# Two buffer changes in a two-layer trunk: narrow PSUM banks for every second pair of v, and GpSimd making both parts of eighteen weights

## The chip, the cores and the metric

The kernel runs on one core of a Trainium2 chip. The metric is device time in microseconds (us) of one execution, from the chip; lower is better. The core has a matrix engine (TensorE, PE in the profile; its weight loads are PEld), VectorE (DVE), ScalarE (ACT), GpSimd (POOL) and a sync engine that issues the DMAs (SP). Each engine runs its own queue in order and waits on semaphores for the others. Matmul results land in PSUM, eight banks of 128 partitions x 512 fp32; GpSimd doesn't touch PSUM in this kernel.

## The reference

The input is one sequence of 1024 tokens with 1024 features, all fp32. Two layers follow each other.

```python
def _dsa_mixer(x, ...):                 # layer 0
    q, c_kv, q_idx, k_idx, w_idx, z = split(x @ w_in)
    c_kv = rmsnorm(c_kv)
    # per block of 128 queries: score all causal keys, keep the best 256
    idx_score = einsum(w_idx, relu(q_idx @ k_idx.T)); sel = top_k(idx_score, 256)
    p = softmax(q_lat . c_kv[sel] - slope * distance)
    return ((p . c_kv[sel]) @ w_uv * silu(z)) @ w_out

def _mlstm_mixer(x, ...):               # layer 1
    qk, v, ig, fg, o, z = split(x @ w_in)
    # causal conv and silu on qk, then a chunked recurrence with gates ig, fg over q, k, v
    return (sigmoid(o) * rmsnorm(h) * silu(z)) @ w_out

# each layer: x = layernorm(alpha * x + mixer(x))
```

## The kernel before

Every large product is made in three passes of a rounded fp32 format (fp32r). `mm3` (lines 58 to 61) multiplies a high part h and a low part l of each operand: h·h, h·l and l·h. The high part is a rounded copy of the fp32 value, the low part is the value minus the high part. So each weight that arrives by DMA is split twice: a copy that makes h, and a subtract that makes l. `split_sb` (line 54) puts the copy on ScalarE and the subtract on VectorE, or on an engine that is given.

`load_w` (line 63) does this for the weights of the first layer: a DMA from the sync queue into `w_st` (line 67, two buffers), a ScalarE copy into `w_h` (line 68, three buffers) and a subtract into `w_l` (line 69, three buffers) on VectorE or, with `pool_l=True`, on GpSimd. `pool_l` is true for eighteen weights of 128x1024: eight for z (`z_unit`), two for the key/value latent (`ckv_a`) and eight for q (`q_unit`). Five others (`w_idx1` and four of `load_u`) use VectorE.

The first layer has three stages that matter here. In the first, TensorE makes the index scores of six query blocks (`scores`), and the z, latent and q projections (`proj_T`). At the same time the top 256 keys of each block are found by a search bit by bit (`sel_step`): for each of 32 bits and each group of blocks, one pass over the scores M counts how many reach a candidate value, and two tiny VectorE instructions (lines 269 and 270) move the candidate. Groups a, b and c (blocks 7, 6 and 5) count on ScalarE (line 253), groups d and e (blocks 4, 3 and 2) on VectorE (line 256). `sel_final` (lines 280 to 308) then turns the scores of each group into a mask in M. The third stage, attention (`soft`, `attend`), reads the masks. Between them `k_unit` and `v_piece` make keys and values of the first pair of heads.

The second layer begins with the v projection. `v_unit` (line 721) makes plain stretches of columns: its weights come in by DMA and are split (`split_sb`), then four pairs of token blocks (the loop over `tp`) are multiplied into PSUM, each block is copied as `vh` (ScalarE, line 758), subtracted as `vl` (VectorE, line 759) and written to DRAM from the two buffers of `VE`. It is called three times: columns 1792 to 2056 (264 wide, gates included), 1024 to 1536 (512 wide) and 1536 to 1792 (256 wide). `v_unit7` makes the other half of v after it.

PSUM has two kinds of tiles: `ps_a` has one bank and four buffers ("narrow"), `ps_y` has two banks and two buffers ("wide"). All plain units of v use `ps_y`. Around them `ps_a` holds the transposes `xt` of the norm (line 590) and the transposed gates `yg` (line 635, two banks, read by lines 640 and 645).

The order on each engine is not written out by hand up to line 1123: a planner places instructions by their dependences, their place in the program and its own estimate of durations, and chooses when a buffer is given out. By hand is only the later part (`manual_schedule`, pairs and the recurrence).

Of the kernel before, what the change touches and what calls it, by code (L numbers as in the profile page):

```python
# [14 lines left out]
AF = mybir.ActivationFunctionType  # L15
# [15 lines left out]
def trunk(ctx, tc, I, out):  # L31
    nc = tc.nc
    PE, DVE, ACT, POOL, SP = nc.tensor, nc.vector, nc.scalar, nc.gpsimd, nc.sync
# [8 lines left out]
    def ps_a(name="pa"):  # L42
        return ps.tile([128, 512], F32, name=name, tag="a", bufs=4)

    def ps_y(name="py"):
        return ps.tile([128, 2, 512], F32, name=name, tag="y", bufs=2)

    def slab(name, dt=F32, shape=(128, 1024)):
        return xp.tile(list(shape), dt, name=name, tag="x", bufs=16)

    def f32(ap):
        return ap.bitcast(F32)

    def split_sb(src, h, l, eng=None):
        ACT.activation(h, src, AF.Copy)  # L55
        (eng or DVE).tensor_tensor(l, src, f32(h), op=OP.subtract)  # L56

    def mm3(o, sh, sl, mh, ml, start, stop):
        PE.matmul(o, lhsT=sh, rhs=mh, start=start, stop=False)  # L59
        PE.matmul(o, lhsT=sh, rhs=ml, start=False, stop=False)  # L60
        PE.matmul(o, lhsT=sl, rhs=mh, start=False, stop=stop)  # L61

    def load_w(src, shape, pool_l=False):
        st = wp.tile(list(shape), F32, name="w_st", tag="st", bufs=2)
        h = wp.tile(list(shape), F32R, name="w_h", tag="wh", bufs=3)
        l = wp.tile(list(shape), F32R, name="w_l", tag="wl", bufs=3)
        SP.dma_start(st[:], src)
        ACT.activation(h[:], st[:], AF.Copy)  # L68
        (POOL if pool_l else DVE).tensor_tensor(l[:], st[:], f32(h[:]), op=OP.subtract)  # L69
        return h, l  # L70

# [54 lines left out]
    for k in range(8):  # L126
        xs = ap_.tile([128, 1024], F32, name="xs", tag="p", bufs=4)
        st = wp.tile([128, 456], F32, name="w_st", tag="st", bufs=2)
        wh = wp.tile([128, 456], F32R, name="w_h", tag="wh", bufs=3)
        wl = wp.tile([128, 456], F32R, name="w_l", tag="wl", bufs=3)  # L130
        h, l = slab("xh", F32R), slab("xl", F32R)
# [17 lines left out]
    def proj_T(src, pool_l=False):  # L149

        wh, wl = load_w(src, [128, 8, 128], pool_l)
        y = ps_y()
        for k in range(8):
            for hf in range(2):
                s = slice(hf * 512, hf * 512 + 512)
                mm3(y[:, hf, :], wh[:, k, :], wl[:, k, :], xh[k][:, s], xl[k][:, s], k == 0, k == 7)
        return y[:].rearrange("p a b -> p (a b)")
# [24 lines left out]
    for c in range(2):  # L182
        y = yq[c][:].rearrange("p a b -> p (a b)")
        stack_q(c, [(y[:, 256:1024], 256, 768)])
    stack_q(2, [(aq[0][0][:, 256:512], 256, 256), (aq[0][1][:, :], 512, 512)])
    y = proj_T(I["w_idx1"])
# [13 lines left out]
    for b in range(2):  # L200
        n = 128 * (b + 1)
# [115 lines left out]
    def ckv_a():  # L317
        w = [load_w(I["w_ckv"][i], [128, 4, 256], True) for i in range(2)]
        for tp in range(4):
            if tp % 2 == 0:  # L320
                ckf.append(ap_.tile([128, 4, 256], F32, name="ckf", tag="z", bufs=2))
            a = ps_a("ck")
            for j in range(2):
                t = slice((2 * tp + j) * 128, (2 * tp + j) * 128 + 128)
                for k in range(8):
                    wh, wl = w[k // 4]
                    mm3(a[:, j * 256:j * 256 + 256], xh[k][:, t], xl[k][:, t], wh[:, k % 4, :],
                        wl[:, k % 4, :], k == 0, k == 7)
            o = (tp % 2) * 2
            ACT.activation(ckf[-1][:, o:o + 2, :], a[:].rearrange("p (j c) -> p j c", j=2), AF.Copy)  # L330
            for j in range(2):
                ACT.activation(a[:, j * 256:j * 256 + 256], ckf[-1][:, o + j, :], AF.Square,
                               accum_out=ckss[:, 2 * tp + j:2 * tp + j + 1])
# [32 lines left out]
    def load_u(p):  # L366
        uw[p] = load_w(I["w_ukv"][p], [128, 2, 2, 256])
# [178 lines left out]
    for k in range(8):  # L546
        st = wp.tile([128, 1024], F32, name="w_st", tag="st", bufs=2)
        SP.dma_start(st[:], I["a_w_out"][k])
        h, l = slab("woh", F32R), slab("wol", F32R)
# [3 lines left out]
    def x2tile(name, dt=F32R):  # L553
        return x2p.tile([128, 4, 512], dt, name=name, tag="x2", bufs=8)
# [13 lines left out]
    for b in range(NB):  # L568
# [7 lines left out]
        y = ps_y("yo")  # L576
        for h, hf in ([(h, hf) for h in range(8) for hf in range(2)] if b < 2 else
                      [(h, hf) for hf in range(2) for h in range(8)]):
                n = slice(hf * 512, hf * 512 + 512)
# [7 lines left out]
        for c4 in range(2):  # L587
# [4 lines left out]
            for c in range(4):  # L592
                k = c4 * 4 + c
# [3 lines left out]
            h, l = (v[:, :, (b % 4) * 128:(b % 4) * 128 + 128] for v in X1[c4][b // 4])  # L597
# [123 lines left out]
    def v_unit(c0, c1, on_slabs):  # L721
        n = c1 - c0
        nv = min(c1, 2048) - c0
        w = []
        g = 1024 // n // 2 * 2 or 2
        for i in range(8 // g):
            st = wp.tile([128, g, n], F32, name="v_st", tag="st", bufs=2)
            SP.dma_start(st[:], I["w_vg"][:, g * i:g * i + g, c0:c1])
            if i < 3 and not on_slabs:
                wh = wp.tile([128, g, n], F32R, name="v_h", tag="wh", bufs=3)  # L730
                wl = wp.tile([128, g, n], F32R, name="v_l", tag="wl", bufs=3)
            else:
                wh, wl = (slab("v_x", F32R, (128, g, n)) for _ in range(2))
                if on_slabs:
                    XT.extend([wh, wl])
            split_sb(st[:], wh[:], wl[:])
            w += [(wh[:, j, :], wl[:, j, :]) for j in range(g)]
        if nv < n:
            G = slab("G", F32, (128, NB, 36))
            GC.append(G)  # L740
            POOL.memset(G[:, :, 4:32], 0.0)
        h, j0 = divmod(c0, 512)
        j0 //= 256
        nj = nv // 256
        js = slice(j0, j0 + nj)
        for tp in range(4):
            y = ps_y("yv")
            for j in range(2):
                tb = 2 * tp + j
                for k in range(8):  # L750
                    xh1, xl1 = (v[:, (tb % 4) * 128:(tb % 4) * 128 + 128] for v in x1[k][tb // 4])
                    mm3(y[:, j, :n], xh1, xl1, *w[k], k == 0, k == 7)
                if nv < n:
                    for i in range(2):
                        DVE.tensor_copy(G[:, tb, 32 * i:32 * i + 4], y[:, j, 256 + 4 * i:260 + 4 * i])
                vh, vl = VE[j]
                yv = y[:, j, :nv].rearrange("p (j n) -> p j n", j=nj)
                ACT.activation(vh[:, js, 0:256], yv, AF.Copy)
                DVE.tensor_tensor(vl[:, js, 0:256], yv, f32(vh[:, js, 0:256]), op=OP.subtract)
                for o, v in ((XH, vh), (XL, vl)):  # L760
                    o += 258 * j0
                    SP.dma_start(X_dram[h, tb, :, o:o + 258 * nj],
                                 f32(v[:, js, :].rearrange("p j n -> p (j n)")))
# [335 lines left out]

    W2 = {}  # L1100
    v_unit(1792, 2056, False)
    gates()
    gate_cols()
    v_unit(1024, 1536, True)
    XT += [slab("T", F32R, (128, 2, 512)) for _ in range(8)]
    right_factors(2)
    right_factors(3)
    right_factors(0)
    right_factors(1)
    v_unit(1536, 1792, False)  # L1110
    bctx.close()
    actx, sctx = ExitStack(), ExitStack()
# [26 lines left out]
    p = pairs[0]  # L1139
    for f in (p.prep0, p.prep1, p.prep2, p.prep3, p.s1, p.s2):  # L1140
        f()
    for n, p in enumerate(pairs[:-1]):
# [4 lines left out]
        if n == 19:  # L1147
            for k in (0, 2):
                st = x2tile("w2_st", F32)
# [318 lines left out]
```

## Time and profile before

| what | value |
|---|---|
| median of three runs | 1577.13 us (1575.67 to 1577.32) |
| profiled execution | 1580.19 us, its span 1578.1 us |
| mean granted TensorE clock | 0.989 |
| busy share of the span | PE 97%, PEld 83%, DVE 75%, ACT 55%, POOL 11% |

The profiled execution is 3.1 us above the median of the three runs, and 2.1 us of it lie outside the span (first to last instruction). "Busy" is the time in which an engine had an instruction under way; instructions overlap a little at their ends. A wait is given by the instruction that waited, the one that released it, and how long the engine sat idle. Times in the rows are us from the span's start.

### The profile page before, as it was taken

Reading aid. Unit: us, or ns where it says so; the run is one execution under the profiler, and the core shown is the slowest. Engines: PE = TensorE matmul, PEld = TensorE weight load, DVE = VectorE, ACT = ScalarE, POOL = GpSimd, SP = SyncE. Lnnn points to the kernel's source line nnn. Section 1 sums busy time; section 2 is a strip of 40 time slices with the busy share of each in tenths; the row PEclk is TensorE's granted clock in tenths of the full one; section 3 lists DMA queues with packets and bytes.
Section 4 is the critical chain, followed back from the end, with each engine's and each line's share of the span. In section 5 each row is a group of like instructions: output and inputs, shape, how many; then the busy total and the mean of one; then the engine's idle time right before and its main releaser. Section 6 shows DMA issues by size and latency. Waiting matters only on the chain.

```text
span 1578.1 us, 22430 instructions
## 1 busy us (share of the span) xinstructions
PE 1537.9 (97%) x8081; PEld 1312.4 (83%) x8081; DVE 1176.6 (75%) x2393; ACT 866.1 (55%) x1554; POOL 177.2 (11%) x158
## 2 busy tenths in 40 slices
PE   9999999999999999999999999999999999999997
PEld 6888888899998888887878888888888778888886
DVE  3569999887873558836788888987776677757876
ACT  3588887576775546222456464646565554344431
POOL 0212112044368300000000000000000000000000
PEclk9999999999999999999999999999999989999999
DMA  5121211111013335245746656574662476676551
GB/s 182 54 80 56 80 41 48 47 32 35 30 54 95 117 129 164 96 154 164 240 158 210 190 184 204 168 232 140 185 209 81 159 266 227 215 249 248 204 197 41
DMA packets 118510, 223.41 MB, mean 142 GB/s; under 512 B 9336, under 2 KB 66040, under 8 KB 114816
## 3 DMA queue, kind: packets, MB, share of 16 engines
q1 hardware_dynamic: 118400, 222.00, 42.8%
q8 instruction: 63, 1.03, 0.3%
q14 instruction: 47, 0.39, 0.1%
HBM read 148.40 MB, written 73.56 MB: 141 GB/s over the span
## 4 chain that ended last, share of the span: by engine, by line
PE 68%; DVE 19%; DMA 6%; ACT 4%; issue 3%; POOL 0%; SPq 0%; DVEq 0%; ACTq 0%; POOLq 0%
PE p L59 6%; PE p L61 6%; PE p L60 6%; PE yo L59 5%; PE yo L61 5%; PE yo L60 5%; DVE junk L256 3%; PE ys L59 2%; PE ys L61 2%; PE ys L60 2%; PE pt L471 2%; DVE M L224 2%; ACT junk L253 1%; DMA f_st<-in_w_vg_dram 1%; PE yl L59 1%
## 5 line engine op out<-in xcount | busy, mean ns | idle before, releaser
L59 PE MATMUL py<-xh,w_h 128*128 128x512 f32 x272 | 106.6, 392 | 1.6 <-ACT w_h L68 1.4
L61 PE MATMUL py<-xh,w_l 128*128 128x512 f32 x272 | 106.4, 391 | 0.0
L59 PE MATMUL yo<-wo,oh 128*128 128x512 f32 (+1 forms) x264 | 104.3, 395 | 2.1 <-ACT oh L55 2.0
L60 PE MATMUL py<-xl,w_h 128*128 128x512 f32 x272 | 106.1, 390 | 0.0
L61 PE MATMUL yo<-wo,ol 128*128 128x512 f32 (+1 forms) x264 | 103.9, 394 | 0.1
L60 PE MATMUL yo<-wo,oh 128*128 128x512 f32 (+1 forms) x264 | 103.8, 393 | 0.0
L59 PE MATMUL p<-x1h,p_h 128*128 128x512 f32 x192 | 75.6, 394 | 0.1
L61 PE MATMUL p<-x1h,p_l 128*128 128x512 f32 x192 | 74.8, 390 | 0.0
L60 PE MATMUL p<-x1l,p_h 128*128 128x512 f32 x192 | 74.8, 389 | 0.0
L56 DVE TENSOR_TENSOR p_l<-p_st,p_h 128x1024 fp32r<-128x1024 f32 x48 | 58.7, 1223 | 17.6 <-ACT p_h L55 17.5
L55 ACT ACTIVATE p_h<-p_st 128x1024 fp32r<-128x1024 f32 x48 | 50.6, 1055 | 32.9 <-PE p L60 26.6
L454 POOL TENSOR_SCALAR p<-p,sm 128x640 f32<-128x640 f32 (+2 forms) x24 | 58.3, 2437 | 70.6 <-DVE sm L453 57.2
L69 POOL TENSOR_TENSOR w_l<-w_st,w_h 128x1024 fp32r<-128x1024 f32 x18 | 44.3, 2466 | 192.8 <-ACT w_h L68 192.8
L55 ACT ACTIVATE p_h<-p_f 128x1024 fp32r<-128x1024 f32 (+1 forms) x48 | 40.4, 842 | 42.7 <-PE ys L60 20.3
L59 PEld LDWEIGHTS py<-xh,w_h 128*128 128x128 f32 x272 | 51.2, 188 | 12.5 <-ACT w_h L68 1.7
L61 PEld LDWEIGHTS yo<-wo,ol 128*128 128x128 f32 x264 | 50.4, 191 | 13.1 <-DVE ol L56 1.1
L59 PEld LDWEIGHTS yo<-wo,oh 128*128 128x128 f32 x264 | 50.3, 191 | 12.5 <-ACT oh L55 3.0
L1030 DVE SCALAR_TENSOR_TENSOR acc<-yq,conv_w,acc 128x1023 f32<-128x1023 f32 (+2 forms) x48 | 60.1, 1277 | 0.0
L61 PEld LDWEIGHTS py<-xh,w_l 128*128 128x128 f32 x272 | 51.3, 189 | 10.3
L60 PEld LDWEIGHTS py<-xl,w_h 128*128 128x128 f32 x272 | 51.2, 188 | 10.3
L55 ACT ACTIVATE Ch<-Cf 128x516 fp32r<-128x516 f32 x56 | 35.6, 635 | 43.7 <-DVE Cf L1270 42.8
L60 PEld LDWEIGHTS yo<-wo,oh 128*128 128x128 f32 x264 | 50.4, 191 | 9.7
(484 smaller groups left out, 5134.8 us busy)
## 6 DMA issues: line engine op xcount, KB each, us to landing
X<-X_dram SPq DMA_DIRECT2D x28, 1156.0 KB, 5.6
f_st<-in_w_vg_dram SPq DMA_DIRECT2D x18, 512.0 KB, 3.7
p_st<-in_w_qk_dram SPq DMA_DIRECT2D x16, 512.0 KB, 4.5
p_st<-in_w_o_dram SPq DMA_DIRECT2D x16, 512.0 KB, 3.7
qk_dram<-acc SPq DMA_DIRECT2D x16, 512.0 KB, 3.4
cqk<-qk_dram SPq DMA_DIRECT2D x16, 512.0 KB, 5.4
p_st<-in_w_z_dram SPq DMA_DIRECT2D x16, 512.0 KB, 3.9
X_dram<-qhl SPq DMA_DIRECT2D x32, 256.0 KB, 3.9
```

Of the source, the lines that this page charges most:

```text
L55: ACT.activation(h, src, AF.Copy)
L56: (eng or DVE).tensor_tensor(l, src, f32(h), op=OP.subtract)
L59: PE.matmul(o, lhsT=sh, rhs=mh, start=start, stop=False)
L60: PE.matmul(o, lhsT=sh, rhs=ml, start=False, stop=False)
L61: PE.matmul(o, lhsT=sl, rhs=mh, start=False, stop=stop)
L69: (POOL if pool_l else DVE).tensor_tensor(l[:], st[:], f32(h[:]), op=OP.subtract)
L224: DVE.scalar_tensor_tensor(M[b][:, o], r[:, :w], wcol[:, b, h:h + 1], M[b][:, o], op0=OP.mult, op1=OP.add)
L253: ACT.activation(j, M[b][:], AF.Sign, bias=f32(cand[:, i:i + 1]), scale=1.0, accum_out=cnt[:, i:i + 1])
L256: DVE.tensor_scalar(j, M[b][:], f32(cand[:, i:i + 1]), None, op0=OP.is_ge, op1=OP.add, accum_out=cnt[:, i:i + 1])
L454: (POOL if b in (4, 6, 7) else DVE).tensor_scalar(p[:, :n], p[:, :n], sm[:, 0:1], None, op0=OP.mult)
L471: PE.transpose(a[:, j * 256 + e * 128:j * 256 + e * 128 + 128], P[e][:, s:s + 128], ident[:])
L1030: DVE.scalar_tensor_tensor(acc[:, j:], y[:, 0:1024 - j], conv_w[:, w, 3 - j:4 - j], acc[:, j:], op0=OP.mult, op1=OP.add)
```

## The change

In `load_w`, where `pool_l` is true, the copy that makes `w_h` moves from ScalarE (an activation with Copy) to GpSimd (a tensor copy); the subtract was there already. In `v_unit`, the second and fourth pair of token blocks take two narrow tiles (`ps_a`) in place of one wide one (`ps_y`). What is computed stays the same.

```diff
@@ load_w
         SP.dma_start(st[:], src)
-        ACT.activation(h[:], st[:], AF.Copy)
+        if pool_l:
+            POOL.tensor_copy(h[:], st[:])
+        else:
+            ACT.activation(h[:], st[:], AF.Copy)
         (POOL if pool_l else DVE).tensor_tensor(l[:], st[:], f32(h[:]), op=OP.subtract)
@@ v_unit
         for tp in range(4):
-            y = ps_y("yv")
+            if tp % 2:
+                y = [ps_a("yv") for _ in range(2)]
+            else:
+                t2 = ps_y("yv")
+                y = [t2[:, j, :] for j in range(2)]
             for j in range(2):
@@ and the uses follow: y[:, j, ...] becomes y[j][:, ...]
```

## Rows read from the trace of the kernel before

**Rows 1.** Page, part 1: busy us (share), instructions.
```profile
PE 1537.9 (97%) x8081; PEld 1312.4 (83%) x8081; DVE 1176.6 (75%) x2393; ACT 866.1 (55%) x1554; POOL 177.2 (11%) x158
```
**Rows 2.** Windows: length, busy us (instructions) of PE PEld DVE ACT POOL, clock, DMA.
```profile
50.00:110.00 60.00, 60.00 (x281) 50.10 (x280) 35.70 (x69) 43.48 (x77) 14.03 (x9) 1.00 0.18 60
110.00:304.00 194.00, 190.74 (x954) 162.44 (x952) 187.39 (x634) 146.97 (x278) 31.76 (x17) 0.99 0.18 58
304.00:500.00 196.00, 193.28 (x1326) 179.31 (x1326) 146.09 (x379) 137.10 (x329) 100.42 (x67) 1.00 0.14 44
575.00:610.00 35.00, 30.41 (x226) 28.49 (x225) 26.08 (x56) 19.66 (x39) 1.33 (x3) 1.00 0.53 167
610.00:685.00 75.00, 74.13 (x434) 64.78 (x433) 57.72 (x72) 28.96 (x39) 0.00 (x0) 1.00 0.35 114
```
**Rows 3.** Timeline of VectorE, then TensorE, where the selection ends: start, us.
```profile
303.21 0.96 DVE L308 SCALAR_TENSOR_TENSOR M<-wide,nd 128x768 f32<-128x768 f32 x1
304.09 0.68 DVE L381 TENSOR_TENSOR kl<-yk,kh 128x512 fp32r<-128x512 f32 x1
...
304.83 0.50 PE L59 MATMUL yk<-ckh,w_h 128*128 128x512 f32 x1 [0.80 <-DVE kl L381]
```
**Rows 4.** Waits of TensorE, 575 to 690: us in total, times, longest.
```profile
PE yv L59 <- DVE vl L759: 5.2, 5, 1.7
```
**Rows 5.** Timeline of TensorE: first and last of those five waits.
```profile
588.88 0.39 PE L59 MATMUL yv<-v_h,x1h 128*128 128x264 f32 x1 [1.70 <-DVE vl L759]
...
639.94 0.50 PE L59 MATMUL yv<-v_x,x1h 128*128 128x512 f32 x1 [0.64 <-DVE vl L759]
```
**Rows 6.** Timeline after v: a weight copy that waits for TensorE, and what follows.
```profile
690.32 1.06 ACT L55 ACTIVATE f_h<-f_st 128x1024 fp32r<-128x1024 f32 x1 [2.09 <-PE v L61]
```
**Rows 7.** Timeline: the first gate transpose into a narrow bank, and the last read.
```profile
592.78 0.27 PE L635 MATMUL yg<-ident,G 128*36 128x128 f32 x1
...
618.62 0.68 ACT L645 ACTIVATE f<-yg,bias 4x512 f32<-4x512 f32 x1
```
**Rows 8.** Groups of instructions on GpSimd by shape: busy us, mean ns, idle before.
```profile
L69 POOL TENSOR_TENSOR w_l<-w_st,w_h 128x1024 fp32r<-128x1024 f32 x18 | 44.3, 2466 | 192.8 <-ACT w_h L68 192.8
...
L454 POOL TENSOR_SCALAR p<-p,sm 128x1024 f32<-128x1024 f32 x8 | 22.8, 2849 | 0.0
...
L704 POOL TENSOR_SCALAR_AFFINE_SELECT Ab<-Ab 128x1024 f32<-128x1024 f32 x4 | 4.3, 1091 | 192.9 <-PE p L61 183.1 <-DMA Ab<-row_dram 9.8
```
**Rows 9.** Group of ScalarE, 110 to 300: the copies into w_h.
```profile
L68 ACT ACTIVATE w_h<-w_st 128x1024 fp32r<-128x1024 f32 x13 | 13.7, 1053 | 2.1 <-issue 2.1
```
**Rows 10.** Timeline of GpSimd and VectorE around one subtract of a weight.
```profile
110.53 0.29 POOL L226 TENSOR_SCALAR_AFFINE_SELECT M<-M 128x128 f32<-128x128 f32 x1 [0.55 <-DVE M L224]
122.01 0.52 POOL L226 TENSOR_SCALAR_AFFINE_SELECT M<-M 128x128 f32<-128x128 f32 x1 [11.19 <-DVE candd L270]
123.77 2.40 POOL L69 TENSOR_TENSOR w_l<-w_st,w_h 128x1024 fp32r<-128x1024 f32 x1 [1.25 <-ACT w_h L68]
...
121.92 0.45 DVE L222 TENSOR_SCALAR M<-r,wcol 128x448 f32<-128x448 f32 x1
...
123.94 2.25 DVE L270 SCALAR_TENSOR_TENSOR canda<-selta,canda 128x1 int32<-128x1 int32 x1
126.12 0.15 DVE L270 SCALAR_TENSOR_TENSOR candd<-seltd,candd 128x1 int32<-128x1 int32 x1
```
**Rows 11.** Windows, line 270 alone: VectorE busy us and instructions, 110 to 304.
```profile
110.00:304.00 194.00, 32.66 (x145) 0.99 0.18 58
```
**Rows 12.** Waits of VectorE, 110 to 304.
```profile
DVE seltc L269 <- ACT junk L253: 3.3, 7, 1.2
```
**Rows 13.** Windows: TensorE's idle stretch and the granted clock after it.
```profile
164.00:172.00 8.00, 4.96 (x19) 3.10 (x18) 8.00 (x34) 7.77 (x16) 1.88 (x1) 0.94 0.04 14
172.00:176.00 4.00, 4.00 (x16) 3.51 (x15) 4.00 (x14) 3.81 (x9) 0.49 (x1) 0.69 0.65 234
```
**Rows 14.** Waits of TensorE, 40 to 320.
```profile
PE py L59 <- ACT w_h L68: 1.4, 1, 1.4
```

More of the change, by code (lines that the diff above doesn't have):

```diff
@@ L751, in v_unit @@
                     xh1, xl1 = (v[:, (tb % 4) * 128:(tb % 4) * 128 + 128] for v in x1[k][tb // 4])
-                    mm3(y[:, j, :n], xh1, xl1, *w[k], k == 0, k == 7)
+                    mm3(y[j][:, :n], xh1, xl1, *w[k], k == 0, k == 7)
                 if nv < n:
                     for i in range(2):
-                        DVE.tensor_copy(G[:, tb, 32 * i:32 * i + 4], y[:, j, 256 + 4 * i:260 + 4 * i])
+                        DVE.tensor_copy(G[:, tb, 32 * i:32 * i + 4], y[j][:, 256 + 4 * i:260 + 4 * i])
                 vh, vl = VE[j]
-                yv = y[:, j, :nv].rearrange("p (j n) -> p j n", j=nj)
+                yv = y[j][:, :nv].rearrange("p (j n) -> p j n", j=nj)
                 ACT.activation(vh[:, js, 0:256], yv, AF.Copy)
```

## The prediction

> **What bounds the kernel now.** I read the page's busy shares first [rows 1]: TensorE is busy 97% of the span, so a change pays only where TensorE stands still, and costs only where it makes TensorE stand still. The windows by stage come next [rows 2]: in 110 to 304 us TensorE idles 194.0 - 190.7 = 3.3 us, but VectorE idles only 194.0 - 187.4 = 6.6 us, and ScalarE is busy 147.0 of 194.0. From 304 on TensorE is full (193.3 of 196.0) and VectorE has room (146.1). So up to 304 two engines run side by side at their limit: TensorE with the projections, VectorE with the selection. The timeline shows where they meet [rows 3]: VectorE writes the last mask from 303.21, then makes kl at 304.09, and TensorE has waited 0.80 us for kl at 304.83. There is no slack at this seam. Whatever makes VectorE later before 304 makes TensorE later, and whatever makes TensorE alone earlier before 304 is lost there, but for the 0.8 us. After it, attention follows TensorE, so that a delay at the seam goes on to the end.
>
> The second place is v. In 575 to 610 TensorE idles 35.0 - 30.4 = 4.6 us, in 610 to 685 another 0.9 us [rows 2]. The waits of TensorE there have one entry: 5.2 us in five waits for vl, the last reader of a PSUM tile of v [rows 4]; the first is 1.70 us at 588.88, the last 0.64 us at 639.94 [rows 5].
>
> **Narrow banks for every second pair of v.** No instruction is added or removed. Matmuls, copies, subtracts and DMAs stay; the tile of a pair comes from another pool. Now the third pair waits until the first has been read; after the change the wide tiles serve the first and third pair and the narrow ones the second and fourth, so that a tile is asked for again later by one pair. One pair is 48 matmuls, and 226 matmuls fill 30.4 us in 575 to 610 [rows 2], so a pair takes about 6 us; that is longer than the longest of the five waits, 1.70 us, and each should vanish. The most to gain is 5.2 us. Does it reach the end? At 690.32 the next weight copy waits 2.09 us for TensorE to be done with a buffer [rows 6], so the work behind v follows TensorE, and the gain goes on. What can be late next is the narrow banks themselves. There are four. The transposed gates take two of them one after the other, the first from 592.78, and the last read of one starts at 618.62 [rows 7], and the last norm transposes hold two more for a part of that time. The fourth pair of the first unit asks for two in this stretch. That can cost between nothing and about as much as the waits that it replaces. I take 4.5 us of the 5.2, with ends of 5.2 gained and 2 lost.
>
> **The copies on GpSimd, what they take away.** In 110 to 300 ScalarE makes thirteen copies of weights, 1.05 us each [rows 9]. One is for `load_u(0)` and stays; twelve of the eighteen go, 12.6 us of work. ScalarE isn't the bound, so this is worth only what VectorE now waits for ScalarE: 3.3 us in seven waits of the group c [rows 12], and at most VectorE's whole idle time of 6.6 us [rows 2]. The six earlier copies lie mostly where VectorE idles 60.0 - 35.7 = 24.3 us of 60 [rows 2]; they may bring its work forward a little, and I allow 2 us. TensorE's wait of 1.4 us for w_h [rows 14] is part of an idle stretch of 8.00 - 4.96 = 3.04 us [rows 13]; it lies before the seam and is lost there.
>
> **What they add.** Each copy now takes GpSimd's time ahead of the subtract. The trace has no tensor copy on GpSimd, so its length is bounded by the nearest rows of 128x1024 [rows 8]: an affine select, one input and one output, takes 1.09 us; a multiplication by one scalar a row, also one input, takes 2.85 us; the subtract itself 2.40 to 2.47. I take 1.09, since the select is nearest in moving one input without arithmetic.
>
> GpSimd has the time (31.8 of 194 busy). The cost is on VectorE. Around the subtract that starts at 123.77 and takes 2.40 us, the update of canda starts at 123.94 and takes 2.25 us, ending with the subtract; its twin candd, right after it, takes 0.15 us [rows 10]. So the subtract holds VectorE. The same shows in the sum of that line: 145 updates take 32.66 us [rows 11], where 145 x 0.15 = 21.8 are their undisturbed length, so 10.9 us on this line alone are holds. Per subtract that is 10.9 / 12 = 0.9 us at least, and 2.1 us in the one shown; I take 1.6 of the 2.4, since other two-input lines are held too. What is left over, some 0.8 us, is free because VectorE is then in an instruction that goes on beside GpSimd; after that it reaches one that doesn't. If the copy holds VectorE alike, it comes first, uses up those free 0.8 us, and everything behind it is hold: each weight costs VectorE a whole copy more, 12 x 1.09 = 13.1 us. Does a one-input instruction of GpSimd exclude VectorE at all? The select at 122.01 took 0.52 us beside a VectorE scaling that began at 121.92 [rows 10], against 0.29 for its like at 110.53, so such instructions do exclude each other.
>
> The Trainium skill's page "SBUF — State Buffer", section "Who interferes with whom", states the rule for it: VectorE with two SBUF inputs and GpSimd reading SBUF need the same port, and whoever comes second is blocked for the whole instruction. By that rule the copy, which reads SBUF, holds VectorE, and the sum is the +1.7 us below; without it, it is that of rival (b). The trace agrees for the subtract [rows 10], and shows no copy. The skill's "GPSIMD Engine Reference", section "Engine selection", says that one-input operations run at about line rate on GpSimd; the select agrees, the multiplication does not; by that rule the copy is the short one and rival (a) falls [rows 8].
>
> Queues: the copy stands in GpSimd's queue ahead of its subtract and, if the planner puts it so, ahead of the affine selects of scores (line 226), for which the selection of a block waits; a copy there delays it by at most 1.1 us. No DMA moves; the sync queue issues the same loads. The copy no longer waits behind counting passes on ScalarE.
>
> **The sum.** At the seam VectorE is later by 13.1 - 6.6 - 2.0 = 4.5 us. TensorE then idles that long more. Where TensorE idled 3.04 us in 164 to 172, the granted clock averaged 0.94 over those 8 us and 0.69 over the next 4 (for a while at the lower of its two levels, 1.2 against 2.4 GHz) [rows 13]: 0.06 x 8 + 0.31 x 4 = 1.7 us, which I add once. Together 4.5 + 1.7 - 4.5 = +1.7 us. Against the profiled execution (1580.19 us, span 1578.1) this would be 1581.9; the median of the runs is 3.1 us lower, 1577.13, and from it the forecast is 1578.8, or 1579.
>
> **The rivals.** (a) The copy is long. If it costs GpSimd what the subtract or the multiplication does, the hold is 12 x 2.40 = 28.8 or 12 x 2.85 = 34.2 us: +17.4 or +22.8 us in all, 1595 to 1600. For it speaks the one multiplication row; against it the select. It decides from about 1.2 us of copy on, where the loss at the seam outgrows any gain in v by more than 0.2%. (b) ScalarE's relief wins: the holds fall where VectorE stands in counting passes, or the copy doesn't hold it. Then VectorE ends earlier, up to the 6.6 us that it idles, TensorE's 3.04 us of idle time and the slow clock behind it (1.7 us) go too, and with 4.5 us in v the change gives -5 to -10 us, 1567 to 1572; I put it at 1571. For it speaks that VectorE's seven waits are all for ScalarE [rows 12] and that weights no longer queue behind counting passes; against it, the 2.25 us hold. (c) The narrow banks run short beside the gates: the gain in v turns into a wait of 2 us. 4.5 + 1.7 + 2 = +8.2, 1585. It decides if a narrow bank is still held when the fourth pair arrives near 600. (d) The planner, whose modelled times change with the copies, orders the first layer anew and the seam shifts by a few us either way; I have no row for that, and it widens every case by about 3 us.
>
> **How the numbers follow.** About 0.2% (3.2 us) is what a measurement of this kernel can tell from no change. My forecast has 48%: 9 of them faster, 21 within, 18 slower (+1.7, spread by the ends of v and by the planner). (a) has 13%, all slower. (b) has 28%: 23 faster, 5 within. (c) has 11%: 8 slower, 3 within. Together faster 0.32, same 0.29, slower 0.39. The forecast's own range is 1573 to 1586. For 8 in 10 it reaches down to 1569, into (b), and up to 1595, to the near end of (a).
>
> **What would show it.** In the profile of the changed kernel: tensor copies on GpSimd near 1.1 us, and behind each a VectorE update that lasts about a whole copy longer than now (3 us where it is 2.25). The last mask (line 308) written some 4 to 5 us later than 304, and a TensorE wait at the first yk or yl of about 5 us. ScalarE 18 copies of 1.05 us lighter. In v the five waits for vl gone or under 1 us together; if waits for xt, yg or lines 640 and 645 stand there, it is (c). The prediction is wrong if the last mask is written before 304, or if GpSimd's copies take over 2 us.

## The result, and the profile of the changed kernel

The changed kernel takes 1607.04 us (median of six runs, 1602.45 to 1609.29) against 1577.22 for the kernel before in the same comparison: a ratio of 1.0186, with a 95% interval from 1.0174 to 1.0198, or 29.8 us slower. The forecast was 1579, its own range ended at 1586, and the one for 8 in 10 at 1595. The profiled execution took 1609.29 us with a span of 1606.8. In the changed file the line numbers behind `load_w` are 3 higher than before, those behind `v_unit`'s loop 7 higher.

The page's busy shares, to be read against [rows 1]:

```profile
PE 1543.2 (96%) x8081; PEld 1316.3 (82%) x8081; DVE 1185.3 (74%) x2393; ACT 849.0 (53%) x1536; POOL 197.6 (12%) x176
```

ScalarE lost eighteen instructions and GpSimd gained them; no engine became the bound. The time is in TensorE's gaps. The same windows as [rows 2]; the stretch of v lies 12 us later now, so its windows move along:

```profile
110.00:304.00 194.00, 183.10 (x882) 154.45 (x881) 187.66 (x620) 129.47 (x256) 45.20 (x28) 0.96 0.16 52
304.00:500.00 196.00, 193.90 (x1319) 179.44 (x1318) 143.32 (x372) 136.43 (x326) 93.10 (x55) 1.00 0.13 41
...
587.00:622.00 35.00, 32.99 (x247) 31.50 (x246) 25.86 (x55) 19.56 (x39) 1.33 (x3) 1.00 0.52 163
622.00:697.00 75.00, 54.25 (x242) 45.12 (x241) 48.48 (x58) 22.21 (x28) 0.00 (x0) 0.84 0.25 84
```

Up to 304 us TensorE idles 10.9 us in place of 3.3, at a granted clock of 0.96 in place of 0.99. Attention is untouched. In the second half of v TensorE idles 20.8 of 75 us, where it idled 0.9, and the clock is 0.84. TensorE's waits, first 40 to 330 us, then 587 to 697, name who was late (sc are the index scores, py the projections; r, zs and qf are ScalarE's copies of such results out of PSUM, its evictions):

```profile
PE sc L218 <- ACT r L223: 4.7, 5, 1.8
PE py L59 <- ACT zs L235: 4.3, 1, 4.3
PE py L59 <- ACT qf L365: 1.9, 1, 1.9
...
PE gt L692 <- ACT f L677: 13.8, 1, 13.8
PE yv L59 <- DVE vl L766: 9.0, 3, 5.6
```

In the kernel before, TensorE waited in 40 to 320 us for no zs, 0.2 us for qf, and for r:

```profile
PE sc L215 <- ACT r L220: 1.7, 3, 0.9
```

Two places, then, and in neither the wait that I forecast. In the first layer three kinds of eviction on ScalarE are late. In v one single wait of 13.8 us appears: `gt`, the transposed gate columns of `gate_cols`, stands in TensorE's queue and waits for the end of the gate chain (f). The timeline of VectorE, where the selection ends, shows the seam [rows 3]:

```profile
304.16 0.96 DVE L311 SCALAR_TENSOR_TENSOR M<-wide,nd 128x768 f32<-128x768 f32 x1
305.04 1.22 DVE L56 TENSOR_TENSOR ql<-qf,qh 128x1024 fp32r<-128x1024 f32 x1
313.24 0.69 DVE L384 TENSOR_TENSOR kl<-yk,kh 128x512 fp32r<-128x512 f32 x1 [6.98 <-ACT kh L383]
```

The last mask is only 0.95 us later than before, not 4 to 5. But kl is 9.15 us later, and VectorE has stood idle for 6.98 us before it: the order at the seam has turned round, VectorE waits there and TensorE is late.

The copies themselves did as forecast (groups on GpSimd, as in [rows 8]):

```profile
L72 POOL TENSOR_TENSOR w_l<-w_st,w_h 128x1024 fp32r<-128x1024 f32 x18 | 45.8, 2545 | 1.4 <-POOL w_h L69 0.3
L69 POOL CAST w_h<-w_st 128x1024 fp32r<-128x1024 f32 x18 | 19.5, 1084 | 155.1 <-PE py L60 78.5 <-PE aq L60 44.7 <-PE ck L61 20.7
```

1.08 us each, where 1.09 was taken from the affine select; rival (a) falls here. The Trainium skill's page "GPSIMD Engine Reference", section "Engine selection", has one-input operations at roughly line rate; this cast agrees (1.08 us, where ScalarE's copy of the same size took 1.05 [rows 9]).

### The profile page after: what moved, and what is told of

It reads as the page before. It is cut to its first block, busy times and chain, and to the rows that moved or that the text cites. A ratio compares the mean times of both kernels' runs of the same rounds, so it can differ in the third digit from the quotient of the medians.

```text
span 1606.8 us, 22441 instructions
## 1 busy us (share of the span) xinstructions
PE 1543.2 (96%) x8081; PEld 1316.3 (82%) x8081; DVE 1185.3 (74%) x2393; ACT 849.0 (53%) x1536; POOL 197.6 (12%) x176
## 4 chain that ended last, share of the span: by engine, by line
PE 73%; DVE 15%; DMA 5%; ACT 4%; issue 3%; POOL 0%; SPq 0%; DVEq 0%; ACTq 0%; POOLq 0%
PE p L59 6%; PE p L61 6%; PE p L60 6%; PE yo L59 5%; PE yo L61 5%; PE yo L60 5%; PE ys L59 2%; PE ys L61 2%; PE ys L60 2%; DVE junk L259 2%; PE pt L474 2%; DMA f_st<-in_w_vg_dram 1%; ACT junk L256 1%; PE py L59 1%; PE py L60 1%
## 5 line engine op out<-in xcount | busy, mean ns | idle before, releaser
L59 PE MATMUL p<-v_x,p_h 128*128 128x512 f32 x144 | 56.8, 394 | 0.0
```

## Experiments

Every kernel ran beside the kernel before on its chip, and ratios are to that.

**One part each (e1, e2).** e1 is the diff of `v_unit` alone, e2 that of `load_w` alone.

> Narrow banks alone, the copies stay on ScalarE. Theory A (two separate losses): the narrow banks move the gates' transposes gt forward in TensorE's queue, which then stands still for the end of the gate chain; this needs no copies, so the stretch of v loses about 19 us here too (13.8 us of wait at gt, the rest the slow clock behind it): 1594 to 1598 us, and the first layer ends when it did before. Rival B (the copies do it all; v is late only because the first layer was): no wait at gt, the five waits for vl gone, about 1573 us.

> Copies alone, all pairs of v on wide tiles. Theory A: the first layer loses what it loses in the changed kernel, about 11 us at the end of the projections, partly late evictions and partly the slow clock, and v is as before: 1586 to 1590 us. Rival B: all or nearly all of the loss, 1600 us or more. Rival C (the first layer's loss is given back in attention): about 1577 to 1580 us.

e1: 1598.13 against 1579.25 us, ratio 1.0122 (1.0109 to 1.0135), +18.9 us. e2: 1590.75, ratio 1.0076 (1.0060 to 1.0093), +11.5 us (differences of medians; by the ratios 19.3 and 12.0; gains and losses of the runs below go by the ratio). Their sum of 30.4 is the whole loss of 29.8: within what the intervals allow, the two parts cost their own and don't meet. Theory A, rival B falls. Waits of TensorE in v, e1, then gt in the timeline of TensorE with the two ends of the chain that feeds it (last read of yg, last f before gt):

```profile
PE gt L689 <- ACT f L674: 13.8, 1, 13.8
PE yv L59 <- DVE vl L763: 8.8, 3, 5.5
...
618.24 0.68 ACT L645 ACTIVATE f<-yg,bias 4x512 f32<-4x512 f32 x1
...
649.74 1.06 ACT L674 ACTIVATE f<-f 4x1024 f32<-4x1024 f32 x1 [21.58 <-DVE f L665]
...
650.94 0.98 PE L689 MATMUL gt<-ident,li 4*128 4x4 f32 x8 [13.80 <-ACT f L674]
```

And of the kernel before, the same f and the same gt:

```profile
651.38 1.06 ACT L674 ACTIVATE f<-f 4x1024 f32<-4x1024 f32 x1 [3.77 <-DVE f L665]
...
655.12 0.66 PE L689 MATMUL gt<-ident,li 4*128 4x4 f32 x8
```

The chain isn't late. Its input is read at 618.24 (before: 618.62 [rows 7]) and its f ends at 649.74 + 1.06 = 650.80, 1.6 us *earlier* than before (652.44). (gt waits for the end of this chain: its first eight transposes read li, which ends beside f, at 650.84.) What changed is where gt stands in TensorE's queue: 198 matmuls of v stood behind it before, 288 stand behind it in e1, so 90 went from ahead of it to behind it. TensorE reaches gt at 650.94 - 13.80 = 637.1 us, 18.0 earlier than before, and everything behind it stands too. In the kernel before, gt started 2.7 us after its f; f is 1.6 us earlier now, so 18.0 - 2.7 - 1.6 = 13.7 of the 13.8 us follow from its place alone. Behind gt in the queue stand 120 matmuls of the 512-wide unit, by the program's order first the 48 of its second pair, the first pair that asks for narrow tiles after gt in the program, and 24 matmuls of the third unit have been taken ahead: the planner gave gt its narrow bank first (that it deals banks in the order of the program is read from this order; no run shows the rule itself). Four windows show what the clock adds:

```profile
631.60:637.20 5.60, 5.49 (x24) 5.19 (x24) 5.57 (x2) 0.00 (x0) 0.00 (x0) 0.50 0.13 47
637.00:652.00 15.00, 1.20 (x11) 1.09 (x11) 14.78 (x13) 1.06 (x1) 0.00 (x0) 0.61 0.01 1
652.00:660.00 8.00, 8.00 (x29) 6.48 (x29) 0.81 (x5) 1.29 (x2) 0.00 (x0) 0.62 0.04 6
660.00:670.00 10.00, 10.00 (x46) 8.29 (x45) 2.08 (x3) 1.80 (x3) 0.00 (x0) 1.00 0.44 160
```

After the idle stretch the granted clock averages 0.62, for most of that window the lower level (1.2 against 2.4 GHz): the first twelve matmuls of yv behind gt take 5.3 us (652.71 to 657.99), the next twelve 2.8, so 2.5 us are lost. The 24 matmuls of the third unit ahead of gt, behind a wait of 5.5 us for vl, ran at the lower level too (0.50): 5.5 us in place of 3.0 at the spacing of 0.12 us that the same matmuls have in the kernel before, some 2.4 lost. So 13.8 at gt, 8.8 - 5.2 = 3.6 more for vl, and 4.9 of clock: 22.3, where 18.9 were measured. Some 3 us must have come back elsewhere; the gain by the narrow banks (e4c below) is of that size, but this was not taken apart.

**gt later (e3, e4, e4c, e5b).** In e3 (both parts) and e4 (narrow banks alone):

```diff
-    gate_cols()
     v_unit(1024, 1536, True)
+    gate_cols()
```

> The changed kernel with gate_cols() called behind v_unit(1024, 1536), so that 120 more matmuls of yv stand ahead of the 16 transposes gt in TensorE's queue. Theory A (what costs is the place of gt in the queue): the wait of 13.8 us at gt and the slow clock behind it go, the first layer's 11 us stay: 1584 to 1589 us. Rival D (narrow banks run short around the gates, the place of gt is only where it shows): the wait moves to yv or yg, and the time stays over 1600 us.

> Narrow banks alone, with gate_cols() called behind v_unit(1024, 1536). Theory A: no wait at gt, and what is left is the gain by the narrow banks, at most the five waits of 5.2 us that go: 1572 to 1576 us, if no other wait of this size comes up in v. Rival D: over 1590 us.

e3: 1585.56 us, ratio 1.0047 (1.0032 to 1.0061), so 22 of the 30 us are gone by moving one call. e4: 1577.00, ratio 0.9988 (0.9977 to 0.9999), 1 us above the range expected. Theory A; rival D falls. e4c puts the call behind the last plain unit; e5b leaves it where e4 has it and uses narrow tiles only where `nv == n`, that is, not in the unit with the gates.

> e4 with gate_cols() behind the last plain unit: the 1.6 us that TensorE waits at gt in e4 go too. If that is all: 1574 to 1577 us. If the tables of the gates, made from gt, are then late for the recurrence, or gt's wait only hid another: 1577 us or more.

> Narrow banks only in the second and third plain unit, so that the gates' transposes yg find their banks as before, and gate_cols() behind the second unit. The yg come some 15 us earlier than in e4 again and gt is ready when TensorE gets there; the first unit keeps its waits for vl (some 3 of the 5.2 us). If the place of yg matters, 1573 to 1576 us; if not, the first unit's waits are back and it is 1577 to 1579 us.

e4c: 1575.37 against 1578.73 us, ratio 0.9978 (0.9967 to 0.9989), the fastest kernel of this study: 3.5 us better than before (1.7 to 5.2). e5b: 0.9997 (0.9988 to 1.0006), no gain that can be told from nothing. Where does e4c's gain come from? Its wait of TensorE in 575 to 690:

```profile
PE yv L59 <- DVE vl L763: 4.4, 2, 2.6
```

And the stretch from the first matmul of the plain units to the first one behind `v_unit7`, in the kernel before, e4c and e5b:

```profile
580.30:768.20 187.90, 176.75 (x953) 150.85 (x952) 133.46 (x189) 73.16 (x108) 1.04 (x2) 0.98 0.48 155
...
581.40:765.70 184.30, 174.49 (x953) 151.17 (x952) 133.54 (x189) 71.97 (x108) 1.05 (x2) 0.98 0.48 157
...
579.70:763.80 184.10, 174.79 (x953) 150.69 (x953) 134.29 (x189) 73.50 (x108) 1.05 (x2) 0.98 0.49 159
```

The waits for vl fell only from 5.2 (five) to 4.4 (two). The stretch is 3.6 us shorter in e4c, 1.3 of them less idle time (11.2 to 9.8); the clock is 0.98 in all three and isn't the gain. Why the same 953 matmuls are busy 2.3 us less was not found. e5b's trace, of its fastest execution, shows the same gain in v, though its median shows next to none, so one trace each doesn't settle what v is worth. And no run moves `gate_cols` with all pairs on wide tiles, so how much of the gain is the place of gt is open.

**Order or hold (e9, e10).** In the first layer the copies could cost in two ways: GpSimd holds VectorE, or the planner, which reckons with the copies, puts the queues in another order. The two can be taken apart, since the order of a queue can be pinned: an ordering edge from each instruction to the next one on its engine, without a wait. e9 has e2's copies and the pinned order of the kernel before on TensorE, VectorE and ScalarE. e10 has the copies on ScalarE, where the planner puts them in between, and e2's order of all else. That the pinning by itself costs nothing is seen in e12 below, which has the same edges (ratio 1.0003).

> The copies alone on GpSimd, as in e2, but the order of the queues of TensorE, VectorE and ScalarE is held to that of the kernel before (ScalarE's without its eighteen copies). Theory H (GpSimd's reads hold VectorE, which makes ScalarE's counting passes and evictions late): the loss of e2 stays, 1587 to 1592 us, and the waits for r and zs with it. Rival O (the planner's new order of the queues makes the loss, the hold is small): 1574 to 1581 us, no wait of 4 us for zs.

> The copies on ScalarE as in the kernel before, but the order of the queues of TensorE, VectorE and ScalarE is held to that of e2 (the eighteen copies placed in between). Theory H: 1576 to 1581 us, as before. Rival O: e2's loss without any copy on GpSimd, 1587 to 1592 us, with the wait for zs near 217 us.

e9: 1582.16 against 1577.96 us, ratio 1.0028 (1.0015 to 1.0041), +4.4, 1 us above the range of rival O. e10: 1587.14, ratio 1.0060 (1.0044 to 1.0077), +9.5, without a single copy on GpSimd. So most of the loss is the new order (rival O), and the hold is real but smaller; together they come to 13.9, where e2 lost 12.0 by its ratio. e10 also carries eighteen copies on ScalarE in an order that was planned without them; e2 against e9, the copies on GpSimd in both, gives the order alone: 12.0 - 4.4 = 7.6 us. TensorE's waits in e10, then in e9:

```profile
PE py L59 <- ACT zs L234: 4.7, 1, 4.7
PE sc L217 <- ACT r L222: 4.4, 4, 1.7
```

```profile
PE sc L218 <- ACT r L223: 4.4, 3, 2.5
PE py L59 <- ACT qf L365: 2.5, 1, 2.5
```

The wait for zs belongs to the order. With the old order the last mask of e9 comes 4.2 us later [rows 3], as the prediction had it (4 to 5), but TensorE waits for r and qf, and not for kl at the first yk:

```profile
307.39 0.96 DVE L311 SCALAR_TENSOR_TENSOR M<-wide,nd 128x768 f32<-128x768 f32 x1
```

**The hold (e11, e12).** Both keep ScalarE's copies and the pinned order of before, and add work on GpSimd ahead of each subtract:

```diff
         if pool_l:
+            POOL.tensor_copy(l[:], st[:])        # e11
+            POOL.memset(f32(l[:]), 0.0)          # e12
```

> The kernel before with one more copy on GpSimd for each of the eighteen weights: the staged weight into w_l, which the subtract then overwrites; ScalarE keeps its copies, and the order of the three other queues is held to that of before. Theory H by the prediction's sum: twelve holds of 1.09 us less the 6.6 us that VectorE idles, 6.5 us later at the last mask, and 1.7 us of clock: 1586 to 1589 us; without a hold 1578 to 1580 us. Half a hold each (the copy falls partly where VectorE goes on): near 1579 to 1581 us.

> As e11, but GpSimd writes zeros into w_l in place of the copy: nothing is read from SBUF. If only GpSimd's reads hold VectorE, 1577 to 1580 us and VectorE's updates beside it keep 0.15 us; if any instruction of GpSimd holds it, as e11, in proportion to its length. What e11 costs over this run is the hold by reading alone.

e11: 1583.36, ratio 1.0034 (1.0024 to 1.0043), +5.4 us, between the cases of whole and of half holds. e12: 1578.60, ratio 1.0003 (0.9994 to 1.0012). The memset is about as long as the copy (groups of e11, then e12):

```profile
L70 POOL CAST w_l<-w_st 128x1024 fp32r<-128x1024 f32 x18 | 19.0, 1056 | 150.8 <-PE py L61 74.1 <-PE aq L61 44.8 <-PE ck L60 17.5
```

```profile
L70 POOL MEMSET w_l<- 128x1024 f32 x18 | 17.2, 954 | 154.7 <-PE py L61 84.9 <-PE aq L61 45.4 <-PE ck L60 16.7
```

17.2 us of GpSimd that reads nothing cost nothing that can be measured (at most 1.9 us by the interval); 19.0 us that read SBUF cost 5. I added up, from the traces up to 308 us, by how much VectorE's instructions beside such an instruction outlast the short ones (the first quartile) of their form, where it is over 0.05 us: 6.7 us beside e11's copies and 7.6 beside e9's, in eleven instructions each, and 3.0 in eight beside e12's memsets. Per copy that is 0.4 us, not 1.09. The Trainium skill's page "SBUF — State Buffer", section "Who interferes with whom", says that VectorE with two SBUF inputs contends with a GpSimd instruction that reads SBUF, not with one that only writes it; the pair e11 and e12 agrees.

**Which order (e14 to e18).** e14 and e15 are e2 with its own order pinned, and the last zs moved 30 and 3 instructions ahead in ScalarE's queue. e16, e17 and e18 are e2 with only some queues pinned to the order of before: TensorE's; ScalarE's and VectorE's; ScalarE's.

> e2 with its own order of the queues, but for one instruction: the last zs, which stands 30 ScalarE instructions behind the counting pass that runs when its product is ready, is moved ahead of them. If this one place makes the wait of 4.3 us and the slow clock behind it (some 3 us): 1582 to 1586 us. If the product behind it waits for something else anyway (its weight, a counting pass): 1588 to 1592 us, as e2.

> e2 with its own order of the queues, but the last zs moved ahead of the three counting passes that stand between the end of its product (near 213 us) and it. If its place makes TensorE's wait of 4.3 us and the slow clock behind it (3.4 us): 1583 to 1587 us. If VectorE's selection, which loses those passes' earliness, or the wait for r sets the end: 1588 to 1592 us.

> e2 with TensorE's queue alone held to the order of the kernel before; ScalarE's and VectorE's are left to the planner. If TensorE's order (fourteen scores in one run, the last z product in two halves around the latent ones) makes the 7 to 8 us between e2 and e9: 1580 to 1585 us, as e9. If it is the order on ScalarE and VectorE: 1587 to 1592 us.

> e2 with ScalarE's and VectorE's queues held to the order of the kernel before, TensorE's left to the planner. If the order of those two (where the evictions stand among the counting passes and their updates) makes the 7 to 8 us: 1580 to 1585 us, as e9. If all three orders are needed together: 1587 us or more.

> e2 with ScalarE's queue alone held to the order of the kernel before. If the evictions' places in ScalarE's queue make the 7 to 8 us by themselves: 1580 to 1585 us; if VectorE's order matters as much: 1587 us or more.

| | us | ratio | 95% interval |
|---|---|---|---|
| e2, the planner's order | 1590.75 | 1.0076 | 1.0060 to 1.0093 |
| e14, zs 30 ahead | 1613.66 | 1.0220 | 1.0206 to 1.0234 |
| e15, zs 3 ahead | 1592.16 | 1.0091 | 1.0074 to 1.0107 |
| e16, TensorE's old order | 1589.72 | 1.0074 | 1.0058 to 1.0090 |
| e17, ScalarE's and VectorE's | 1582.01 | 1.0022 | 1.0012 to 1.0032 |
| e18, ScalarE's | 1605.57 | 1.0179 | 1.0160 to 1.0198 |

e14 rests on a misreading: the product that ends at 184 us is only the first half of the last z, the second half follows the latent ones, and ScalarE stood 29.7 us at the moved zs. In e15 the wait for zs goes (0.8 us left), and another takes its place; the waits of TensorE in e15, e16 and e18:

```profile
PE py L59 <- ACT qf L365: 6.7, 3, 4.0
PE sc L218 <- ACT r L223: 5.0, 5, 2.1
PE py L59 <- ACT zs L235: 0.8, 1, 0.8
```

```profile
PE py L59 <- ACT qf L365: 6.2, 5, 3.0
PE sc L218 <- ACT r L223: 4.1, 3, 2.2
```

```profile
PE py L59 <- ACT qf L365: 21.0, 2, 14.9
```

So it isn't the place of zs alone, and not TensorE's order. e17 comes back to e9: the order on ScalarE and VectorE together makes the 7 to 8 us. ScalarE's evictions (r, zs, qf) stand in one queue with the counting passes, each of which waits for a VectorE update. That the two queues therefore have to fit each other is argued from the program; e18, where ScalarE keeps the old order and VectorE a new one, is worse than either, which fits. VectorE's old order alone wasn't run, and which of the many changed places is the dear one was not found.

**Both parts, mended (e13).** Copies on GpSimd, narrow banks, `gate_cols()` as in e4, the three queues pinned to e4's order.

> Both parts of the change, with gate_cols() behind v_unit(1024, 1536) as in e4, and the queues of TensorE, VectorE and ScalarE held to the order of e4 (the eighteen copies on GpSimd). If the losses are the place of gt, the new order of the first layer, and a hold of 4 to 5 us, and add up: e4's 2.3 us gained and e9's 4.4 lost, 1578 to 1582 us, so 25 us or more of the changed kernel's loss go with no copy and no bank moved back. If the copies and the narrow banks meet in some further way: 1585 us or more.

e13: 1583.21 against 1578.73 us, ratio 1.0022 (1.0011 to 1.0034), 1 us above the range expected. 25 of the 30 us are gone with no part of the change undone; the copies still cost more than the narrow banks bring.

## Why the prediction was wrong

**The gain in v: the sum near, its mechanism not.** Forecast were 4.5 us; with gt out of the way e4c gains 3.5 (1.7 to 5.2). But "each should vanish" was wrong: 4.4 us of waits for vl stay, in two, where 5.2 were. So the nearness is luck, and what the gain is made of stays open.

**The narrow banks: the step that failed.** The prediction asked who else holds narrow banks, named yg and xt [rows 7], and bounded the cost by the waits replaced ("as much as"), 2 us in rival (c). It left out the third user, gt, and looked for a bank that is *held*, where the loss came from a bank that is given out *in program order*, as read from e1's queue: pairs of v now had to stand behind gt, and gt behind the gate chain. The bound could have been read from the trace of before: gt started 2.7 us after its f (652.44 to 655.12), so it could move ahead by that much only; each us more is a us that TensorE stands. This step was sized at 2 us and cost 18.9.

**The planner: named, and far too small.** Rival (d) had "a few us either way", 3 us on every case, with no row behind it. The order alone cost 7.6 us (e2 against e9) or 9.5 (e10). A guess without a row was the second term that was mis-sized.

**The hold: right in sum, by luck.** With the order held (e9) the last mask moved by 4.2 us, 4.5 forecast, and the time by 4.4, where the seam and the clock were to cost 6.2. But its terms were off, and their errors cancel. Each of twelve copies was to hold VectorE for its whole 1.09 us, 13.1 in all; 7.6 were measured beside all eighteen, 5.9 of them beside the twelve from 121 us on: only eleven VectorE instructions beside the eighteen copies outlast their form. And ScalarE's relief was to fill all 6.6 us that VectorE idled; in e9 VectorE is busy 188.46 us of 110 to 304 in place of 187.39, so 1.1 us. In the changed kernel itself the hold hardly shows at the mask (0.95 us), because the new order by itself writes it earlier: in e10, without a copy on GpSimd, it starts at 300.98, in e2, with the copies, at 303.26, and before at 303.21.

**The seam** held in one half: a delay there goes on to the end (kl was 9.15 us late, and e2 as a whole lost 11.5). But the delay came from ScalarE's evictions, which the prediction had only as relieved (rival (b)), in e9 too, where TensorE waits 4.4 us for r and 2.5 for qf; the wait of 5 us at the first yk appears in no run. And its test "wrong if the last mask is written before 304" looked at the wrong engine.

## What to carry to other kernels

A change of buffers or engines is also a change of the queues: list every user of a pool whose tiles it takes, in program order, and ask where the planner will put each one's producer; a small transposition that waits for a long chain stalls a whole in-order queue if it moves ahead of the work that covered it. Read from the trace of before how long before its turn such an instruction was ready, since that slack is the price list. Where a planner is at work, pin the order to tell the cost of an instruction from the cost of the new order, both ways round.

## What the runs showed of the hardware

A memset of 128x1024 fp32 on GpSimd takes 0.95 us, about as long as a copy of that size (1.06), and yet leaves the time unchanged (e12). VectorE isn't quite free beside it: of the eight instructions that outlast their form there four are the one-input selte (128x2, 0.15 us else), and two of the others are candb right behind one of these. In e12, a memset and what runs beside it:

```profile
208.99 0.95 POOL L70 MEMSET w_l<- 128x1024 f32 x1 [0.48 <-ACT w_h L68]
...
209.09 0.15 DVE L272 SCALAR_TENSOR_TENSOR candb<-seltb,candb 128x1 int32<-128x1 int32 x1
209.20 0.76 DVE L271 TENSOR_SCALAR selte<-cnte 128x2 int32<-128x2 f32 x1
```

The two-input update candb runs in 0.15 us beside the memset; the one-input selte lasts 0.76, to the memset's end. Beside a copy that reads, in e11, such a two-input update is held:

```profile
164.99 1.04 POOL L70 CAST w_l<-w_st 128x1024 fp32r<-128x1024 f32 x1 [0.54 <-PE py L61]
...
165.03 1.01 DVE L272 SCALAR_TENSOR_TENSOR candd<-seltd,candd 128x1 int32<-128x1 int32 x1
```

And one input doesn't set a price on GpSimd: the cast takes 1.05 to 1.08 us, the multiplication by a scalar of the same size 2.85 [rows 8].
